# A low-rank adapter forward pass: the last software-queue store cut in three, and all software stores issued between casts

## The chip, the cores and the metric

The kernel runs on one core of one Trainium2 chip. The metric is device time in microseconds (us) of one launch. The kernel before took 161.09 us, the median of three runs (160.76 to 161.21).

## The reference

`x` has 16 x 2048 = 32,768 rows of 256 float32 values. The output has the same shape:

```
y = x_flat @ W                                   # W: 256 x 256
lora_out = ((x_flat @ lora_A) * lora_E) @ lora_B # rank 16
y = y + scale * lora_out                         # scale = 1.0
```

Since the adapter is linear, it can be folded into the weights once: `weff = W + lora_A @ diag(lora_E * scale) @ lora_B`. What is left is one product of 32,768 x 256 with 256 x 256. 33.55 MB of `x` come in and 33.55 MB of `y` go out.

## The kernel before

**Tiling.** The rows are cut into four chunks (0 to 3) of 8,192 rows. In a chunk each of the 128 partitions holds 64 consecutive rows (1 KB each) of `x`, so a whole chunk is 64 KB in every partition. An SBUF buffer named `ring` has three homes of that size. Chunk 3 uses the home of chunk 0 again, and a chunk's results overwrite its inputs in place.

**Transfers.** `sync_program` (line 142) goes through the list `ORDER` (line 18) on SyncE's queue, which is one of the hardware-driven queues and is called q1 in the profile. ("L", c, s, e) loads rows s to e of every partition of chunk c (line 155), and ("S", c, s, e) stores them (line 160). A load into a used home first waits for the stores that empty it (line 154). A store first waits for the count `s_done` (line 159). Here the stores are called by chunk: S0 (in two parts), S1, S2, S3. S2 covers only rows 2 to 62 of each partition's 64.

**Software stores.** The first two and last two rows of every partition of chunk 2 are left to GpSimd's software-driven queue, q0 in the profile. The helper `share` (line 163) stores them for a slice of partitions. `SHARES` (line 37) has three slices: partitions 108 to 112 (5 partitions), 0 to 107 (108 partitions) and 113 to 127 (15 partitions). A partition gives two pieces of 2 KB. GpSimd issues these stores at the end of its program (lines 198 to 200), after its last cast and a drain. All three add to one semaphore, `shared_stored`, and SyncE waits for it at line 161, after it has issued S3. The rest of the program's end (a barrier and the clearing of semaphores) follows, and the last wait of all, for S1, S2 and S3 to have landed, stands at line 308.

**Compute.** A cast (GpSimd, line 194) turns eight rows of every partition into bfloat16, in one of two `stage` buffers. There are 32 casts: numbers 0 to 7 are chunk 0, 8 to 15 chunk 1, 16 to 23 chunk 2 and 24 to 31 chunk 3. TensorE works in 64 groups of four rows: `turn` (line 243) transposes a group of a `stage` buffer into PSUM, VectorE copies that to SBUF (line 240), `multiply` (line 266) multiplies with `weff`, and ScalarE copies the product from PSUM into `ring` (line 217).

**Order around the change.** Cast n waits until TensorE has room for it (line 193: `s_room`, raised at the start of every second `multiply`). The first cast of chunk 2 also waits for the first part of S0 to have landed (lines 187 to 189). `s_done` (raised near the end of each `multiply`) is what SyncE waits for before a store. `(SHARED + 1) * ROWS // CG + NY` in line 198 is 50, which is the value that S2 waits for too: two groups past the last group of chunk 2.

Of the kernel before, what the change touches and what calls it, by code (L numbers as in the profile page):

```python
# [7 lines left out]
P = 128  # L8
# [5 lines left out]
ROWS = 64  # L14
# [19 lines left out]

SHARED = 2
END_ROWS = 2
SHARES = (slice(108, 113), slice(0, 108), slice(113, P))

HELD = (2, 0)
HOLDERS = (("S", 0, 0, 40),)  # L40
# [3 lines left out]
CG = 4  # L44
# [4 lines left out]
NS, NX, NT, NY = 2, 2, 2, 2  # L49
# [5 lines left out]
def kernel(  # L55
# [46 lines left out]
    shared_stored = sem("shared_stored")  # L102
# [12 lines left out]
    s_done = sem("rows_done")  # L115

    def rows(c, s, e):
        at = c % N_HOMES * ROWS
        return ring[:, at + s:at + e, :]

    sync, gpsimd, scalar, vector, tensor = nc.sync, nc.gpsimd, nc.scalar, nc.vector, nc.tensor
# [20 lines left out]
    def sync_program():  # L142
        for n, op in enumerate(ORDER):
# [14 lines left out]
            else:  # L158
                sync.wait_ge(s_done, -(-(c * ROWS + e) // CG) + NY)
                sync.dma_start(out=y_chunks[c, :, s:e, :], in_=at_home).then_inc(stored.get(op, stored_rest), 16)  # L160
        sync.wait_ge(shared_stored, 16 * len(SHARES))

    def share(engine, p, landed):
        def ends_of(at):
            return at[p].rearrange("p (q b) k -> p q b k", b=END_ROWS)[:, :: ROWS // END_ROWS - 1, :, :]

        engine.dma_start(out=ends_of(y_chunks[SHARED]), in_=ends_of(rows(SHARED, 0, ROWS))).then_inc(landed, 16)  # L167

    def gpsimd_program():
        gpsimd.memset(ident[:], 0.0).then_inc(s_ident, 1)  # L170
        gpsimd.wait_ge(s_ident, 1)
        gpsimd.affine_select(  # L172
            out=ident[:],
            in_=ident[:],
            compare_op=ALU.not_equal,
            fill=1.0,
            base=0,
            pattern=[[-1, P]],
            channel_multiplier=1,
        ).then_inc(s_ident, 1)  # L180
        n_casts = N_CHUNKS * ROWS // CAST
        for n in range(n_casts):
            c, b = n * CAST // ROWS, n * CAST % ROWS
            for op, landed in loaded.items():
                if op[1:3] == (c, b):
                    gpsimd.wait_ge(landed, 16)
            if (c, b) == HELD:
                for op in HOLDERS:
                    gpsimd.wait_ge(stored[op], 16)
            if n == 1:  # L190
                gpsimd.wait_ge(s_weff, 1)
            if n >= NS:
                gpsimd.wait_ge(s_room, n - NS + 1)  # L193
            gpsimd.tensor_copy(out=stage[n % NS][:], in_=rows(c, b, b + CAST)).then_inc(s_stage[n % NS], 1)  # L194

        gpsimd.wait_ge(s_room, n_casts - NS + 1)
        gpsimd.drain().then_inc(s_stage[n_casts % NS], 1)
        gpsimd.wait_ge(s_done, (SHARED + 1) * ROWS // CG + NY)
        for p in SHARES:
            share(gpsimd, p, shared_stored)  # L200

    def scalar_program():
        for name, to, of in (
# [108 lines left out]
    with tc.tile_critical(no_gpsimd_drain=True):  # L312
        sync_program()
        gpsimd_program()
        scalar_program()
        vector_program()
        tensor_program()
# [35 lines left out]
```

## Time and profile before

| what | value |
|---|---|
| median of 3 runs | 161.09 us (160.76 to 161.21) |
| the profiled execution's own time | 161.41 us |
| its span, from first to last instruction | 160.1 us |
| granted TensorE clock, mean | 0.823 |
| HBM read and written | 33.85 MB and 33.55 MB |
| mean DMA rate over the span | 421 GB/s |
| PE, ACT, POOL, DVE busy | 60%, 41%, 40%, 29% |
| 32 casts on GpSimd | 60.6 us busy, 1896 ns each |
| 3 software-store issues on GpSimd | 2.0 us, 675 ns each on average |

The span is the time from the first to the last instruction of one profiled execution, and that execution took 1.3 us more by the device's clock. In the views, q1 is SyncE's queue, q0 GpSimd's software queue, and an engine's name with a q behind it (SPq) is its sequencer, which waits and issues. "Landing" is the time from the issue of a transfer to its last completion.

### The profile page before, as it was taken

How to read it: one execution, taken by the hardware profiler on the slowest of the kernel's cores; microseconds unless marked ns; L12 is line 12 of the kernel's file. 1: busy time of each engine (PE TensorE's matmuls, PEld its weight loads, DVE VectorE, ACT ScalarE, POOL GpSimd, SP SyncE). 2: the span in 40 equal slices, each digit the busy share in tenths (PEclk: the TensorE clock that was granted, in tenths of full speed). 3: DMA queues.
4: the chain of work that ended last, by engine and by line, in shares of the span. 5: the costliest groups of instructions: out<-in, count | busy, mean ns of one | idle time of the engine just before them, and what ended most of it. 6: DMA issues, size and time to landing. Idle time of an engine off the chain costs nothing.

```text
span 160.1 us, 2042 instructions
## 1 busy us (share of the span) xinstructions
PE 95.3 (60%) x782; PEld 83.3 (52%) x782; DVE 46.1 (29%) x67; ACT 66.3 (41%) x66; POOL 63.3 (40%) x41
## 2 busy tenths in 40 slices
PE   2749999999999910000799999999993000000000
PEld 1235899999999900000699999999992000000000
DVE  0113355555555510000155555555551000000000
ACT  3000577777777730000077777777775000000000
POOL 1044676777767100003676768686850000000000
PEclk9999999999999985555599999999999555555555
DMA  7999999999979997989999999996997998999965
GB/s 270 426 442 436 411 446 434 475 401 401 598 311 524 442 344 328 481 348 442 430 461 393 475 434 401 524 491 295 524 462 308 481 484 354 480 432 390 523 295 248
DMA packets 2449, 67.41 MB, mean 421 GB/s; under 512 B 512, under 2 KB 528, under 8 KB 784
## 3 DMA queue, kind: packets, MB, share of 16 engines
q1 hardware_dynamic: 2016, 66.60, 97.2%
q0 software_dynamic: 224, 0.52, 0.9%
q10 hardware_dynamic: 208, 0.28, 0.5%
q14 instruction: 1, 0.01, 0.0%
HBM read 33.85 MB, written 33.55 MB: 421 GB/s over the span
## 4 chain that ended last, share of the span: by engine, by line
PE 41%; DMA 32%; POOL 2%; ACT 1%; issue 0%; SPq 0%; ACTq 0%; POOLq 0%
DMA out_dram<-ring 27%; PE psum_y L271 26%; PE psum_xt L251 14%; DMA ring<-in_x_dram 5%; POOL stage L194 2%; PE psum_y L297 1%; ACT ring L217 1%; SPq L146 0%; ACTq L217 0%; POOLq L193 0%
## 5 line engine op out<-in xcount | busy, mean ns | idle before, releaser
L217 ACT COPY ring<-psum_y 128x1024 f32 x64 | 64.8, 1013 | 54.3 <-PE psum_y L271 54.3
L194 POOL CAST stage<-ring 128x2048 bf16<-128x2048 f32 x32 | 60.6, 1896 | 52.8 <-DMA out_dram<-ring 22.1
L271 PE MATMUL psum_y<-weff,xt 128*128 128x256 bf16 x512 | 68.5, 278 | 0.0
L240 DVE COPY xt<-psum_xt 128x1024 bf16<-128x1024 bf16 x64 | 44.3, 691 | 62.9 <-PE psum_xt L251 62.9
L251 PE MATMUL psum_xt<-ident,stage 128*128 128x128 f32 x260 | 41.3, 283 | 23.4 <-POOL stage L194 23.4
L271 PEld LDWEIGHTS psum_y<-weff,xt 128*128 128x128 bf16 x512 | 51.3, 100 | 6.0
L251 PEld LDWEIGHTS psum_xt<-ident,stage 128*128 128x128 f32 x260 | 31.6, 146 | 26.3 <-issue 25.2
L283 PE MATMUL psum_y<-ident 128*128 128x512 f32 x4 | 3.8, 1101 | 2.9 <-POOL ident L172 2.9
L283 PEld LDWEIGHTS psum_y<-ident 128*128 128x128 f32 x4 | 1.2, 324 | 3.9 <-POOL ident L172 2.9
L167 POOL DMA_DIRECT2D out_dram<-ring x3 | 2.0, 675 | 1.5 <-PE psum_y L271 1.5
L222 DVE TENSOR_SCALAR stage<-psum_y,e_sb 16x256 f32<-16x256 f32 x1 | 0.5, 472 | 7.2 <-PE psum_y L289 7.2
L211 ACT ACT_TABLE_LOAD x1 | 1.3, 1283 | 2.1 <-SPq L312 2.1
L297 PE MATMUL psum_y<-stage 16*128 16x256 f32 x4 | 2.1, 670 | 0.0
L231 DVE COPY xt<-psum_xt 128x1024 bf16<-128x1024 bf16 x1 | 0.7, 692 | 3.8 <-PE psum_xt L251 3.8
L297 PEld LDWEIGHTS psum_y<-stage 16*128 16x128 f32 x4 | 1.2, 319 | 0.5 <-issue 0.3
L234 DVE TENSOR_TENSOR weff<-stage,psum_y 128x512 bf16<-128x512 f32 x1 | 0.7, 686 | 1.4 <-PE psum_y L297 1.4
L289 PEld LDWEIGHTS psum_y<-ident,a_sb 128*16 128x16 f32 x2 | 0.3, 137 | 1.2 <-issue 1.2
L170 POOL MEMSET ident<- 128x128 f32 x1 | 0.2, 205 | 1.7 <-SPq L312 1.7
L289 PE MATMUL psum_y<-ident,a_sb 128*16 128x128 f32 x2 | 0.6, 421 | 0.0
L172 POOL TENSOR_SCALAR_AFFINE_SELECT ident<-ident 128x128 f32<-128x128 f32 x1 | 0.3, 283 | 0.2 <-POOL ident L170 0.2
L211 ACT COPY one<-ident 128x1 f32<-128x1 f32 x1 | 0.2, 191 | 0.0
L334 POOL MEMSET const-float32-0.0<- 128x1 f32 x1 | 0.1, 93 | 0.2 <-issue 0.2
(3 smaller groups left out, 0.3 us busy)
## 6 DMA issues: line engine op xcount, KB each, us to landing
ring<-in_x_dram SPq DMA_DIRECT2D x4, 4096.0 KB, 24.6
out_dram<-ring SPq DMA_DIRECT2D x1, 7680.0 KB, 37.1
ring<-in_x_dram SPq DMA_DIRECT2D x2, 3072.0 KB, 17.0
out_dram<-ring SPq DMA_DIRECT2D x1, 5120.0 KB, 43.0
out_dram<-ring SPq DMA_DIRECT2D x1, 3072.0 KB, 42.7
ring<-in_x_dram SPq DMA_DIRECT2D x1, 2048.0 KB, 7.9
out_dram<-ring POOLq DMA_DIRECT2D x1, 432.0 KB, 31.3
stage<-in_W_dram ACTq DMA_DIRECT2D x1, 256.0 KB, 2.8
```

What stands on the lines that cost most here:

```text
L167: engine.dma_start(out=ends_of(y_chunks[SHARED]), in_=ends_of(rows(SHARED, 0, ROWS))).then_inc(landed, 16)
L194: gpsimd.tensor_copy(out=stage[n % NS][:], in_=rows(c, b, b + CAST)).then_inc(s_stage[n % NS], 1)
L211: scalar.copy(out=one[:], in_=ident[:, :1])
L217: scalar.copy(out=to, in_=psum_y[i % NY][:]).then_inc(s_free[(i + NY) % UNROLL], 1)
L231: vector.tensor_copy(out=xt[0][:], in_=psum_xt[0][:].bitcast(BF16)).then_inc(s_xt[0], 1)
L234: vector.tensor_add(out=weff[:], in0=w_sb, in1=psum_y[1][:, :KT, :]).then_inc(s_free[0], 1)
L240: vector.tensor_copy(out=xt[g % NX][:], in_=psum_xt[g % NT][:].bitcast(BF16)).then_inc(s_xt[g % UNROLL], 1)
L251: ins = tensor.transpose(psum_xt[i % NT][:, b, :], words[:, at * CG + b, :], ident[:])
L271: ins = tensor.matmul(psum_y[i % NY][:, b, :], xt[i % NX][:, b, t::KT], weff[:, t, :], start=(t == 0), stop=(t == KT - 1),)
L283: ins = tensor.matmul(psum_y[1][:, :2, :], ident[:], ident[:, None, :].to_broadcast([P, 4, P]), start=True, stop=True)
L289: ins = tensor.transpose(psum_y[0][:R, t, :P], a_sb[:, t, :], ident[:])
L297: ins = tensor.matmul(psum_y[1][:, t, :], ate[:, t, :], b_sb, start=True, stop=True)
```

## The change

`SHARES` gets five slices in place of three: the slice of the last 15 partitions is cut into three slices of 5. The stores keep their order: 5 partitions, 108 partitions, then 5, 5 and 5. They leave the end of GpSimd's program and go into its loop over casts: after cast 26 (the third of chunk 3) GpSimd waits for `s_done` to reach 50, and after each of casts 26 to 30 it issues one store. The wait of line 161 follows the number of slices, so it now asks for 80 in place of 48.

```
-SHARES = (slice(108, 113), slice(0, 108), slice(113, P))
+SHARES = (slice(108, 113), slice(0, 108), slice(113, 118), slice(118, 123), slice(123, P))
+FIRST_SHARE = 26
...
             gpsimd.tensor_copy(out=stage[n % NS][:], in_=rows(c, b, b + CAST)).then_inc(s_stage[n % NS], 1)
+            if n == FIRST_SHARE:
+                gpsimd.wait_ge(s_done, (SHARED + 1) * ROWS // CG + NY)
+            if 0 <= n - FIRST_SHARE < len(SHARES):
+                share(gpsimd, SHARES[n - FIRST_SHARE], shared_stored)
 
         gpsimd.wait_ge(s_room, n_casts - NS + 1)
         gpsimd.drain().then_inc(s_stage[n_casts % NS], 1)
-        gpsimd.wait_ge(s_done, (SHARED + 1) * ROWS // CG + NY)
-        for p in SHARES:
-            share(gpsimd, p, shared_stored)
```

## The prediction

> **What bounds the kernel now.** I read the page first: the slices and the queues.
>
> ```profile
> span 160.1 us, 2042 instructions
> ...
> DMA  7999999999979997989999999996997998999965
> ...
> q1 hardware_dynamic: 2016, 66.60, 97.2%
> q0 software_dynamic: 224, 0.52, 0.9%
> q10 hardware_dynamic: 208, 0.28, 0.5%
> ```
>
> The queues' packets fill 97.2 + 0.9 + 0.5 = 98.6% of 16 engines' span; no compute engine is above 60%. The DMA engines are the bound, and only 1.4% of 160.1 us, 2.2 us, is idle on the mean engine. Most of the low digits are packets over 2 us long, booked in one slice. The stretches of the end show it better (columns: length, then busy time of PE, PEld, DVE, ACT and POOL, clock, DMA share, GB/s).
>
> ```profile
> 123.00:139.00 16.00, 0.00 (x0) 0.00 (x0) 0.00 (x0) 0.00 (x0) 0.00 (x0) 0.53 1.00 429
> 139.00:155.00 16.00, 0.00 (x0) 0.00 (x0) 0.00 (x0) 0.00 (x0) 0.00 (x0) 0.50 1.02 435
> 155.00:160.00 5.00, 0.00 (x0) 0.00 (x0) 0.00 (x0) 0.00 (x0) 0.00 (x0) 0.50 0.49 211
> ```
>
> After 123 us nothing computes, and the DMA share is 1.00 and 1.02: full. What is on the queues there, and when it lands, comes from the DMA issues after 100 us (the last line is S3, issued at 122.84):
>
> ```profile
> out_dram<-ring SPq DMA_DIRECT2D x1, 7680.0 KB, 37.1
> out_dram<-ring POOLq DMA_DIRECT2D x1, 432.0 KB, 31.3
> out_dram<-ring POOLq DMA_DIRECT2D x1, 60.0 KB, 35.5
> out_dram<-ring POOLq DMA_DIRECT2D x1, 20.0 KB, 9.6
> out_dram<-ring SPq DMA_DIRECT2D x1, 37.2
> ```
>
> S2 is issued at 103.05 and lands 37.1 later, at 140.1. S3 is issued at 122.84, so it stands 17 us behind S2 in SyncE's queue before its own 20 us of packets run, and lands at 160.05, the end. The software stores, issued from 117.72, land at 127, 150 and 155. Last, the waits of SyncE after 100 us:
>
> ```profile
> SPq L146 <- DMA out_dram<-ring: 31.5, 1, 31.5
> ...
> SPq L308 <- SPq L308: 3.8, 1, 3.8
> ```
>
> The 31.5 us are the wait for the software stores (it ends at 154.7 us). After it comes the program's closing work, done at 156.3, and then 3.8 us of waiting for S3. So the software stores are not the end even now.
>
> **The trace's packet records** tell more. From 8 us on, each of the 16 engines starts a packet as the last one ends; I find no gap over 0.1 us. A 64 KB packet takes 2.418 us, one of 60 KB 2.267, one of 4 KB (both pieces of a partition) 0.159. The engines' last packets end between 158.3 and 159.7 us: one straggler at 159.7, which was already about 0.3 us behind at the first load (8.3) and fell 0.42 more behind at 99.7, the next at 159.1. The straggler's completion ends the kernel.
>
> **What the Trainium skill says.** *DMA: Bandwidth & Descriptors*, "Queues, rings and completion order": an engine goes round its queues packet by packet. The trace agrees: a 4 KB software packet stands after each SyncE packet. The same page, "Why a DMA increments its semaphore by 16 and not by 1": a software store of P partitions runs on the largest divisor of P up to 16, on consecutive engines from a cursor that moves on. The trace agrees: five engines have a data packet of the first store, twelve have nine of the 108-partition store, four have empty 8-byte packets instead, fifteen have one of the last. *Perfetto Trace Analysis*, "DMA Instruction — SWDGE (GPSIMD)": the recorded end of a software issue is when its descriptors are written, so it is GpSimd's cost. *SBUF — State Buffer*, "Who interferes with whom": a VectorE operation in a 2-port mode shuts GpSimd out of its port. The three issues of before ran at 564, 688 and 773 ns between VectorE copies, so no such block shows.
>
> **The change part by part.**
>
> 1. *Bytes per engine.* By the cursor, the first store is on engines 0 to 4, the 108 on 5 to 15 and 0, so 15 go on 1 to 15. After: 1 to 5, 6 to 10, 11 to 15. Partition 113 + j stays on engine 1 + j. Data packets per engine are unchanged: engines 1 to 4 have 2, the others 10. Zero.
>
> 2. *Two more stores.* The software queue's 224 packets are 128 data, 48 completions (3 x 16) and 48 empty ones (11 + 4 x 9 + 1). After: 128 + 80 + (11 + 36 + 33 = 80) = 288. The 64 extra at 9 ns over 16 engines: 64 x 0.009 / 16 = 0.04 us, on the path. Added.
>
> 3. *Moved DMAs.* The five stores' packets now go between those of S1 and S2 rather than S2 and S3. The first lands at about 103.2 + 9.6 = 113, the 108 at 105.8 + 31.3 = 137, the last at some 142. S1 and S2 land later by the packets let through first, at most 10 x 0.159 = 1.6 us an engine, most likely 0.6. Nobody waits for either before the end. Engines that are full do the same packets in another order: zero. This needs SyncE's queue never to run dry, which the next step checks.
>
> 4. *GpSimd.* The casts of chunk 3 show what room there is:
>
> ```profile
> 101.22 1.90 POOL L194 CAST stage<-ring 128x2048 bf16<-128x2048 f32 x1 [0.72 <-PE psum_y L271]
> 103.84 1.90 POOL L194 CAST stage<-ring 128x2048 bf16<-128x2048 f32 x1 [0.72 <-PE psum_y L271]
> 106.53 1.90 POOL L194 CAST stage<-ring 128x2048 bf16<-128x2048 f32 x1 [0.79 <-PE psum_y L271]
> ```
>
> Cast 26 is the first of these, ending at 103.12. The new wait is for 50, which released S2's issue at 103.05, so it costs nothing. The queued casts 27 to 31 each get one issue ahead: 0.56 to 0.77 us, and some 0.1 of dispatch, against 0.72 idle. So each pushes GpSimd by about 0.1, 0.5 us in all at most. TensorE needs cast 26 only at 104.54 (its transposes in the chain): 1.4 us after it was ready. That cover takes the 0.5: compute ends at 121 to 122 as before.
>
> 5. *S3's cover.* Were compute late, S3's issue would be. S2's first engine completes at 138.3; a small load shows 2.3 us from issue to landing, so S3 may be issued up to 138.3 - 2.3 = 136.0, or 13.2 us late, free. Without this cover every us of delay counts in full.
>
> 6. *The end.* The closing work now follows at about 142 to 144, and the last wait grows from 3.8 to some 16 us. It was hidden by S3 and stays so: zero.
>
> Sum: +0.04 us on the profiled execution: 161.41 to 161.45, span 160.1. That execution was 0.3 above the median of the runs, so on the median 161.09 + 0.04 = **161.1 us**.
>
> **The unknown.** The trace doesn't show software packets beside S1 while compute runs, nor what another interleaving does to slow packets. There are such: one of engines 1 to 4 takes 0.16 more on each of nine packets from 100 to 121 us, 1.4 in all; three others of the four lose 0.6 to 0.9 each from 136 to 149. Now they have a lead of 8 x 0.155 = 1.2 us for it, having eight data packets less. Bounds: if the straggler catches up, -0.6 (159.7 to 159.1); if an engine without a lead is hit, +0.6 to +1.4. I take zero, since the straggler's lag predates 103.
>
> **The rivals.**
>
> - *GpSimd starves (slower).* If an issue c is long among casts, compute is late by 5(c - 0.72) - 1.4, and S3 decides once this passes 13.2: c above 3.6 us, five times the 0.675 shown. At c = 4.5: 17.5 - 13.2 = +4.3, 165.4 us. The three measured issues, with VectorE running, speak against it; that none stood between casts is for it. Chance 0.03.
> - *Slow packets hit an engine without a lead (slower).* +0.6 to +1.4: 161.7 to 162.5. For it: such packets are in the trace. Against: seen mostly where an engine had a lead. Chance 0.09.
> - *The end gets more even (faster).* The straggler loses its lag: 160.5. Bounded by 0.6. Chance 0.07.
> - *The move does little, or the software stores are late after all* (the wait is met late, or packets queue up to S3): with some 16 us before the closing work binds, 161.1 too. Chance 0.05.
>
> **How the numbers follow.** Forecast 0.76; with the last rival, 0.81 for no change; slower 0.12, faster 0.07. Within 0.3% (0.48 us) is about what a measurement of this kernel can't tell from no change. The forecast alone spans 160.7 to 161.5, as the runs of before do. The range takes in the faster case and the milder end of the slow packets: 160.5 to 161.8.
>
> **What would show it.** Right: five issues of 0.5 to 0.8 us on GpSimd between casts, its idle time there near nothing; 288 packets on the software queue; S3 issued at 122 to 124; DMA share 1.0 from 123 to 155; the last wait some 16 us. Wrong: S3 issued after 136, gaps on the DMA engines, a 64 KB packet's time well above 2.42 us on the engine that ends last, or closing work after S3.

## The result, and the profile after

The changed kernel takes 167.9 us (median of five runs, 167.7 to 168.0) against 161.18 us for the kernel before in the same comparison. The ratio is 1.042, 95% interval 1.0404 to 1.0436. The prediction said 161.1 us and no change, so it was wrong. The profiled execution took 167.7 us with a span of 166.4 us, where the kernel before had 161.41 and 160.1. So 6.3 us have to be found in the span. Of all executions reported here one was far off (266.62 us, one of ten of the last experiment's kernel, for no known reason) and is left out of its ratio.

The page shows where to look first:

```profile
span 166.4 us, 2044 instructions
...
DMA  7999998989699799899998999969979991099965
...
q1 hardware_dynamic: 2016, 66.60, 93.5%
q0 software_dynamic: 288, 0.53, 0.9%
```

The same 66.60 MB now fill 93.5% of the engines' span rather than 97.2%, and slice 35 of 40 is a plain 0. The bound resource stands still there, which it never did before. The stretches put numbers to it (length, busy time of PE, PEld, DVE, ACT and POOL, clock, DMA share, GB/s), first for the kernel after:

```profile
122.00:138.00 16.00, 0.00 (x0) 0.00 (x0) 0.00 (x0) 0.00 (x0) 0.00 (x0) 0.56 1.05 447
138.00:146.00 8.00, 2.79 (x12) 1.91 (x12) 0.69 (x1) 1.01 (x1) 0.00 (x0) 0.50 0.33 136
146.00:166.00 20.00, 0.00 (x0) 0.00 (x0) 0.00 (x0) 0.00 (x0) 0.00 (x0) 0.50 0.85 367
```

The same eight microseconds in the kernel before:

```profile
138.00:146.00 8.00, 0.00 (x0) 0.00 (x0) 0.00 (x0) 0.00 (x0) 0.00 (x0) 0.50 1.00 426
```

From 138 to 146 us the DMA share falls from 1.00 to 0.33. The packet records name no engine, but after 8 us they fall into 16 chains in which a packet starts as the last one ends, one chain an engine. Each chain has one gap here, of 6.1 to 7.1 us, between its last packet of S2 or of the software stores and its first packet of S3. That accounts for the loss. Odder still, TensorE, VectorE and ScalarE do work in this stretch, some 20 us after compute ended in the kernel before. The chain of waits says what they had waited for:

```profile
118.85 0.44 PE psum_xt L253 x4
119.29 0.12 PE psum_y L273
119.41 21.36 POOLq L202
140.77 0.14 issue
140.91 1.09 PE psum_xt L253 x4
141.99 1.72 PE psum_y L273 x8
...
143.83 1.01 ACT ring L219
```

For 21.36 us TensorE stands behind GpSimd's line 202, `gpsimd.drain().then_inc(s_stage[n_casts % NS], 1)`. The call asks GpSimd to finish what it was given before, and then raises a semaphore. Its one instruction, in the kernel after:

```profile
L202 POOLq DRAIN  x1: 23946/23946/23946, 116.8 to 116.8; - x1
```

and in the kernel before, where it is line 197:

```profile
L197 POOLq DRAIN  x1: 46/46/46, 116.9 to 116.9; - x1
```

The same drain starts at the same time and takes 23,946 ns rather than 46. It ends at 140.76 us, 0.26 us after the last completion of the five software stores (140.50). Its increment lets TensorE do one more transposition of `stage` (line 251 of the kernel before, whose result nobody needs), and the program has that transposition stand ahead of the last `multiply`. So the last group of chunk 3 is some 21 us late, and with it `s_done`, and with that S3. The waits of SyncE after 100 us show it, first before, then after:

```profile
SPq L160 <- PEq L305: 19.4, 1, 19.4
```

```profile
SPq L161 <- PEq L307: 41.7, 1, 41.7
...
SPq L310 <- SPq L310: 19.0, 1, 19.0
```

SyncE waits 41.7 us rather than 19.4 for the count that releases S3, and issues S3 at 144.96 instead of 122.84. The engines had run out of other packets at 138.8 to 139.7. S3 then has the engines to itself and lands 21.4 us later, at 166.34:

```profile
out_dram<-ring SPq DMA_DIRECT2D x1, 7680.0 KB, 37.2
out_dram<-ring POOLq DMA_DIRECT2D x1, 432.0 KB, 29.7
out_dram<-ring POOLq DMA_DIRECT2D x4, 20.0 KB, 28.2
out_dram<-ring SPq DMA_DIRECT2D x1, 21.4
```

The part of GpSimd's queue that the prediction did look at behaves as it said:

```profile
101.13 1.90 POOL L195 CAST stage<-ring 128x2048 bf16<-128x2048 f32 x1 [0.72 <-PE psum_y L273]
103.23 0.69 POOL L168 DMA_DIRECT2D out_dram<-ring  x1 [0.21 <-issue]
103.92 1.90 POOL L195 CAST stage<-ring 128x2048 bf16<-128x2048 f32 x1
105.76 0.79 POOL L168 DMA_DIRECT2D out_dram<-ring  x1
```

The issues take 0.57 to 0.79 us and fit between the casts. The last cast starts at 114.23 here and at 114.33 in the kernel before.

### The profile page after: what moved, and what is told of

It is laid out like the page before. It is cut to its first block, busy times and chain, and to the rows that moved or that the text cites. A ratio compares the mean times of both kernels' runs of the same rounds, so it can differ in the third digit from the quotient of the medians.

```text
span 166.4 us, 2044 instructions
## 1 busy us (share of the span) xinstructions
PE 97.0 (58%) x782; PEld 84.2 (51%) x782; DVE 46.1 (28%) x67; ACT 66.3 (40%) x66; POOL 64.2 (39%) x43
## 3 DMA queue, kind: packets, MB, share of 16 engines
q1 hardware_dynamic: 2016, 66.60, 93.5%
## 4 chain that ended last, share of the span: by engine, by line
PE 40%; DMA 30%; POOLq 13%; POOL 2%; ACT 1%; issue 0%; SPq 0%; ACTq 0%
DMA out_dram<-ring 26%; PE psum_y L273 25%; PE psum_xt L253 14%; POOLq L202 13%; DMA ring<-in_x_dram 5%; POOL stage L195 2%; PE psum_y L299 1%; ACT ring L219 1%; SPq L147 0%; ACTq L219 0%; POOLq L194 0%
## 5 line engine op out<-in xcount | busy, mean ns | idle before, releaser
L273 PE MATMUL psum_y<-weff,xt 128*128 128x256 bf16 x512 | 69.5, 281 | 0.0
L253 PE MATMUL psum_xt<-ident,stage 128*128 128x128 f32 x260 | 42.0, 286 | 43.8 <-POOL stage L195 23.0
L168 POOL DMA_DIRECT2D out_dram<-ring x5 | 3.2, 641 | 0.2 <-issue 0.2
```

What stands on the lines that cost most here:

```text
L253: ins = tensor.transpose(psum_xt[i % NT][:, b, :], words[:, at * CG + b, :], ident[:])
L273: ins = tensor.matmul(psum_y[i % NY][:, b, :], xt[i % NX][:, b, t::KT], weff[:, t, :], start=(t == 0), stop=(t == KT - 1),)
```

## The experiments

The theory after the two traces, called the drain theory below: GpSimd's drain waits until every software store issued ahead of it has landed, and the last TensorE group waits for the increment on that drain. Rivals: the software packets between those of S1 and S2, or the issues between casts, cost the time; the larger number of stores does; or a drain among stores is dear by itself.

### The increment without the drain

```
-        gpsimd.wait_ge(s_room, n_casts - NS + 1)
-        gpsimd.drain().then_inc(s_stage[n_casts % NS], 1)
+        gpsimd.wait_ge(s_room, n_casts - NS + 1).then_inc(s_stage[n_casts % NS], 1)
```

> The changed kernel, with GpSimd's last drain replaced by a bare semaphore increment at the same place. Drain theory (the drain waits until the software stores issued ahead of it have landed, and TensorE's last group waits for its increment): S3 issued at about 122.7 us instead of 145, DMA engines without a gap, 161.1 us, within 0.3% of the kernel before. Traffic theory (software packets between those of S1 and S2, or issues between casts, are what costs): 167 to 168 us still.

Measured: 161.21 us, ratio 1.0001 (0.9986 to 1.0016), span 159.8. S3 is issued at 123.64, and the engines have no gap where they stood still:

```profile
138.00:146.00 8.00, 0.00 (x0) 0.00 (x0) 0.00 (x0) 0.00 (x0) 0.00 (x0) 0.50 0.92 398
146.00:158.00 12.00, 0.00 (x0) 0.00 (x0) 0.00 (x0) 0.00 (x0) 0.00 (x0) 0.50 1.01 438
```

(The 0.92 is how packets of 2.4 us are booked, to the stretch in which they start; the packet records have them back to back.) All five stores are still issued between the casts, and their packets still go among those of SyncE's stores. Neither the traffic nor the issues cost anything that can be measured. The whole 6.7 us went with one drain. From the start of cast 26 to the issue of S3 it is 21.6 us here (102.03 to 123.64) as in the kernel before (101.22 to 122.84), so the issues between the casts didn't make compute later.

### The drain kept, but watched by nobody

```
+        gpsimd.wait_ge(s_room, n_casts - NS + 1).then_inc(s_stage[n_casts % NS], 1)
+        gpsimd.drain()
```

These two lines stand in the place of the two that the first experiment removed.

> The changed kernel, with the increment ahead of the drain, so that nobody waits for the drain. Drain theory: the drain still takes some 24 us (116.8 to 140.7) and costs nothing: 161.1 us. A rival, that a draining GpSimd holds up the DMA engines themselves: 167 to 168 us.

Measured: 161.21 us, ratio 1.0001 (0.9982 to 1.0019). The drain is even longer here:

```profile
L202 POOLq DRAIN  x1: 30309/30309/30309, 117.6 to 117.6; - x1
```

It ends at 147.93, again just after the last software completion (147.67), and costs nothing. So a waiting drain doesn't hold up the DMA engines; what costs is the increment queued on it. The expected 24 us were too short, since S3's packets now stand between the last stores' packets and these land at 147.7 rather than 140.5.

### The cut undone, the move kept

```
-SHARES = (slice(108, 113), slice(0, 108), slice(113, 118), slice(118, 123), slice(123, P))
+SHARES = (slice(108, 113), slice(0, 108), slice(113, P))
```

> The changed kernel with the cut undone: three stores (5, 108 and 15 partitions) after casts 26 to 28, the drain in its place. Drain theory: the last store lands at about 140 as with five, so the drain ends at about 140 to 141 and the time is 167 to 168 us, ratio 1.038 to 1.044. If the number of stores were what counts (0.64 us an issue, more completions): 2 us or more under 167.9.

Measured: 167.36 us, ratio 1.0379 (1.0337 to 1.0421). The drain ends at 140.48, after the last completion at 140.30. Of the 6.7 us of the change, the move alone explains 6.2. Two stores fewer are worth 0.5 us by the medians, not 2, and the intervals of the two ratios overlap. The traces show half of it: S3 is issued at 144.68 rather than 144.96.

### The move undone, the cut kept

```
-SHARES = (slice(108, 113), slice(0, 108), slice(113, P))
+SHARES = (slice(108, 113), slice(0, 108), slice(113, 118), slice(118, 123), slice(123, P))
```

in the kernel before, with all five stores at the end.

> The kernel before with the cut alone: five stores, all issued at the end, after the drain. Drain theory: the drain takes 0.05 us, nothing waits for the stores but the closing work, 161.1 to 161.2 us (0.04 us for 64 more small packets). If more stores cost: slower by over 0.5 us.

Measured: 163.89 us, ratio 1.0161 (1.013 to 1.0193). This was a miss. It can't be the drain, which takes 46 ns. SyncE's waits after 100 us show another thing:

```profile
SPq L146 <- DMA out_dram<-ring: 36.8, 1, 36.8
SPq L160 <- PE psum_y L271: 20.1, 1, 20.1
SPq L160 <- PEq L305: 19.4, 1, 19.4
SPq L348 <- PEq L348: 1.5, 2, 1.2
```

The wait for the software stores is 36.8 us rather than 31.5, and the wait of line 308 for S3 (3.8 us in the kernel before) is gone from the list. The stores end at 160.06, S3 at 159.89, and the closing work now follows in the open until 162.32. The landings of the five stores tell why: 127.4, 149.8, 154.6, 159.4 and 160.1. Each small store behind the first two costs 4.8 us. In the packet records, a store puts two packets on each engine: one of data (or, where it has none, an empty one of 8 bytes) and one for the completion. Each stands behind one 2.42 us packet of SyncE's queue. If a round is one packet of each queue, a store takes two rounds, 4.8 to 5.0 us. The fifth is quick only because S3's packets have run out.

### Four stores at the end

```
-SHARES = (slice(108, 113), slice(0, 108), slice(113, P))
+SHARES = (slice(108, 113), slice(0, 108), slice(113, 121), slice(121, P))
```

> The kernel before with the last 15 partitions in two stores (8 and 7), so four stores, all at the end. Theory from the run with five at the end (on each DMA engine every store puts one completion packet, and here one data or empty packet, and each of these waits for one 2.4 us packet of SyncE's queue): the landings follow at 127, 150, 154.6 and 159.4 us, the last 4.8 us after that of before, and the closing work of about 2 us ends at 161.2 to 161.6: ratio 1.008 to 1.013. If five at the end was slow for another reason (512 KB cut into stores of 5 partitions, or GpSimd's issues): no more than 0.5 us from the kernel before, or about half of the 2.8 us.

Measured: 163.59 us, ratio 1.0151 (1.0136 to 1.0167). The landings are 127.3, 149.6, 154.4 and 159.5, as two rounds a store have it, and the closing work ends at 161.6:

```profile
out_dram<-ring POOLq DMA_DIRECT2D x1, 432.0 KB, 30.4
out_dram<-ring POOLq DMA_DIRECT2D x1, 32.0 KB, 34.5
out_dram<-ring POOLq DMA_DIRECT2D x1, 28.0 KB, 38.9
```

The landing times and the span met the expectation. The total did not quite: the profiled execution took 1.9 us beyond its span (163.49 against 161.6), where the kernel before takes 1.3. The run with five has 1.8 (164.09 against 162.3). Both end on the closing work rather than on the last store. Both also have a packet of 8 KB on the queue q14 (kind "instruction") that ends 0.8 to 1.1 us after the span, where in the kernel before it ends 0.6 us ahead of the span's end. Whether that is the 0.5 us outside the span, no run here shows.

### The stores just ahead of the drain, at the end

```
         gpsimd.wait_ge(s_room, n_casts - NS + 1)
-        gpsimd.drain().then_inc(s_stage[n_casts % NS], 1)
         gpsimd.wait_ge(s_done, (SHARED + 1) * ROWS // CG + NY)
         for p in SHARES:
             share(gpsimd, p, shared_stored)
+        gpsimd.drain().then_inc(s_stage[n_casts % NS], 1)
```

This is the kernel before with two statements exchanged.

> The kernel before with its three stores issued just ahead of the drain rather than behind it, all else at the end as before. Drain theory: issued at about 117, the last store lands some 29 to 38 us later (S3 no longer stands between its packets), so the drain ends at 146 to 155, S3 is issued 4.2 us after that and lands 21.4 later: 173 to 182 us. If the stores' place between casts were the cause: 161.1 us, since no cast follows them here.

Measured: 167.56 us (two executions), ratio 1.0405 (1.0384 to 1.0425). No cast stands behind a store here, and the time is within 0.4 us of the changed kernel's: the place between the casts is not the cause, the place ahead of the drain is. The drain ends at 140.55. The expected 173 to 182 us were wrong, and instructively so. Once S2 has run out (its engines complete at 138.3 to 139.6), nothing stands between the software packets any more, and what would have taken 10 us more takes one: the 108-partition store lands 21.6 us after its issue rather than 31.3, and the last at 140.4. The stall ends itself soon after the engines have nothing else to do. That fits with this kernel, the one with three stores moved and the changed one lying within 0.6 us of each other.

### Fewer stores ahead of the drain

Two runs change how long the drain waits. In the first, only the stores of 5 and of 108 partitions go between the casts and the other three are issued behind the drain:

```
-            if 0 <= n - FIRST_SHARE < len(SHARES):
+            if 0 <= n - FIRST_SHARE < 2:
                 share(gpsimd, SHARES[n - FIRST_SHARE], shared_stored)
 
         gpsimd.wait_ge(s_room, n_casts - NS + 1)
         gpsimd.drain().then_inc(s_stage[n_casts % NS], 1)
+        for p in SHARES[2:]:
+            share(gpsimd, p, shared_stored)
```

> The changed kernel with only the first two stores (5 and 108 partitions) between casts; the other three are issued behind the drain. Drain theory: the drain ends when the 108-partition store has landed, at about 135.6; S3 is issued 4.2 later, at 139.8, just too late to be covered by S2 (done at 139.3 to 139.7): some 1 us of gap on the DMA engines, 162.0 to 162.8 us. If the drain waited for a time by itself, or for the number of stores: about 165 to 168 us.

Measured: 162.59 us, ratio 1.0095 (1.0078 to 1.0112). The 108-partition store lands at 135.65 and the drain ends at 135.79:

```profile
L202 POOLq DRAIN  x1: 17612/17612/17612, 118.2 to 118.2; - x1
```

S3 goes out at 139.98, and the engines' gaps are 0.7 to 2.1 us. In the second run the slices are also changed, so that the store behind the first has 72 partitions and lands sooner:

```
+SHARES = (slice(108, 113), slice(0, 72), slice(113, 117), slice(72, 108), slice(117, P))
```

> As the run with 113 partitions ahead, but the second store has 72 partitions (6 packets on each of 12 engines rather than 9), and the other 51 partitions follow behind the drain in three stores. Drain theory: the 72-partition store lands at about 128, the drain ends there, S3 is issued at about 132.3, which S2 covers by 7 us: no gap on the DMA engines, 161.1 to 161.3 us, although the drain still takes some 11 us. If any drain of many us costs its length: 164 us or more.

Measured: 161.81 us, ratio 1.0045 (1.0028 to 1.0061). The drain ends at 128.89, after the landing at 128.75:

```profile
L202 POOLq DRAIN  x1: 11310/11310/11310, 117.6 to 117.6; - x1
```

S3 goes out at 133.09, ten microseconds late, and there is no gap on the engines: covered, as expected. Yet the time is 0.45% over the kernel before, which was not expected. The next run asks whether that came through S3's wait for the drain. In the kernel of this second run:

```
-        gpsimd.wait_ge(s_room, n_casts - NS + 1)
-        gpsimd.drain().then_inc(s_stage[n_casts % NS], 1)
+        gpsimd.wait_ge(s_room, n_casts - NS + 1).then_inc(s_stage[n_casts % NS], 1)
+        gpsimd.drain()
```

> The run with 77 partitions ahead of the drain, with the increment given ahead of the drain, so that S3 no longer waits for it and goes out at about 123. If the 0.45% of that run came through the drain: ratio 0.998 to 1.002. If they came from its stores' other layout on the DMA engines (slow packets, one engine with more of them): 1.003 to 1.006 as there.

Measured: 161.80 us, ratio 1.0039 (1.0025 to 1.0053), with S3 out at 124.13. So the residue doesn't come of S3's wait for the drain. It belongs to what these two kernels share: the layout of the stores, and the last three of them issued at about 130 us, behind the drain. Which of the two, no run shows. Their packet records have more slow packets: beyond their usual times, the packets of both queues after 100 us lose 12.2 us summed over 16 engines here and 11.7 in the run before, against 4.8 in the kernel before and 4.7 in the first experiment. About half of this is in the 4 KB packets of the software stores (6.2 and 5.4 us, against 1.1 and 1.2). The 7 us more are some 0.45 us an engine, by estimate, and the residue is 0.6 to 0.7 us. What makes packets slow was not found.

### The drain ahead of the first store

```
             if n == FIRST_SHARE:
                 gpsimd.wait_ge(s_done, (SHARED + 1) * ROWS // CG + NY)
+                gpsimd.drain()
...
-        gpsimd.wait_ge(s_room, n_casts - NS + 1)
-        gpsimd.drain().then_inc(s_stage[n_casts % NS], 1)
+        gpsimd.wait_ge(s_room, n_casts - NS + 1).then_inc(s_stage[n_casts % NS], 1)
```

> The changed kernel with the drain moved ahead of the first store (after cast 26), and the bare increment at the end. Drain theory: with no software store under way the drain takes about 0.05 us, and the time is 161.1 us. If the drain is dear by itself among casts: over 161.6 us.

Measured: 161.19 us, ratio 1.001 (1.0 to 1.002). The drain among the casts, with no software store under way, takes 134 ns:

```profile
L198 POOLq DRAIN  x1: 134/134/134, 104.4 to 104.4; - x1
```

### The runs side by side

| kernel | last landing ahead of the drain | drain ends | S3 issued | S3 landed | median |
|---|---|---|---|---|---|
| before | none | 116.96 | 122.84 | 160.05 | 161.18 |
| 77 partitions ahead | 128.75 | 128.89 | 133.09 | 160.53 | 161.81 |
| 113 partitions ahead | 135.65 | 135.79 | 139.98 | 161.37 | 162.59 |
| three stores moved | 140.30 | 140.48 | 144.68 | 166.07 | 167.36 |
| stores, then drain, at the end | 140.38 | 140.55 | 144.75 | 166.14 | 167.56 |
| changed kernel | 140.50 | 140.76 | 144.96 | 166.34 | 167.90 |
| drain watched by nobody | 147.67 | 147.93 | 123.46 | 160.02 | 161.21 |

In every line with a store ahead, the drain ends 0.14 to 0.26 us after the last landing. In the five lines where S3 waits for it, S3 goes out 4.2 us later: the transposition, the last `multiply`, the copy by ScalarE. (The granted clock of that stretch is 0.50 in the changed kernel, and the transposition takes 1.09 us there rather than 0.44.) In the last four of these, where S3 comes after S2 has run out, it lands 21.4 us after its issue. No kernel here beats the one before; the first, second and last experiments equal it.

## Why the prediction was wrong

**Step 4 failed, in its last sentence: "compute ends at 121 to 122 as before".** It named what is queued behind the moved issues, casts 27 to 31. But the drain of line 197 is queued there as well. In the kernel before it stood ahead of the three issues, in the changed one behind the five. It was priced at nothing by silence, although its 46 ns were measured with no software store under way. The runs put in its place: a drain behind a software store waits for that store's landing. It ended at 140.76 us, S3 went out 22.1 us late, and the time grew by 6.7 us.

**Step 3 failed with it: "Nobody waits for either before the end"** was right for S1 and S2, but the software stores themselves got a waiter, the drain, and through it TensorE and S3.

**Step 5 was right as a mechanism and nearly as a size.** It said that S3's issue may slip to 136.0, 13.2 us, for nothing. Issued at 133.09 it left no gap, at 139.98 gaps of 0.7 to 2.1 us. The first packets of S3 start 0.83 us after its issue (145.79 against 144.96), not the 2.3 us taken from a small load's landing, so by an estimate from this trace (138.8 less 0.83) the cover reaches to about 138. The slip was 22.1 us. The first rival, too, had the place right ("compute is late", "S3 decides once this passes 13.2"), but its cause wrong: the issues took 0.57 to 0.79 us, and none came near 3.6.

**Steps 1, 2 and 4 were right as far as they went.** There are 288 packets on the software queue. The wait for 50 cost nothing, and the issues took the time that step 4 gave them. With the drain's increment given freely, the very same stores at the very same places take 161.21 us, ratio 1.0001. So the forecast of no change holds for what it summed; the +0.04 us itself is too small to be told from nothing, as the interval is about 0.25 us to either side.

**Step 2 was right about load and left out latency.** By the prediction two more stores add 0.04 us of work to an engine, but each store behind others takes two rounds of 2.4 us. In the first experiment the last store landed at 147.75, not at "some 142" as step 3 had it. In the change itself little of this was left, since S2's packets had run out: the last landing was at 140.50 against 140.30 with three stores, and the medians differ by 0.5 us. At the end of the program the two stores are worth 2.8 us, since there the closing work loses its cover.

**Step 6, that the closing work stays hidden, was right,** but the 19.0 us of the last wait are no proof of its "some 16", since they come of a late S3. In the first experiment the last wait is 9.9 us, as the last store lands later than step 3 had it. The slow packets of "The unknown" did not decide; more of them than before appeared, beside a cost of 0.4%, only in the two runs with another layout. Two small misreadings of the prediction changed nothing: the three runs of the kernel before span 160.76 to 161.21 us (161.41 with the profiled execution), not 160.7 to 161.5, and its three software issues (117.72 to 119.73) ran in part at the same time as VectorE copies (118.12 to 118.81, 119.43 to 120.12), not between them.

## What to carry to other kernels

When an instruction that starts a transfer moves, look at what it moves past that waits for transfers, a drain above all, and then at who waits for that: a drain of 46 ns is a measurement of what was under way ahead of it. Where a drain is used only to carry a semaphore increment, put the increment on a plain semaphore instruction, as the first experiment does, or issue the stores behind the drain, as the kernel before does. And count a small store beside a busy queue in rounds as well as in bytes: with 2.4 us packets on the other queue, a store of one packet an engine waited for two of them.

## What the runs showed of the hardware

- GpSimd's drain waits for the landing of the software stores that it has issued, and ended 0.14 to 0.26 us after their last completion in seven kernels. It doesn't wait for SyncE's stores: with 77 partitions ahead it ended at 128.89, while S2 landed at 140.36. Without any under way it took 46 ns, or 134 ns right after a cast.
- A software store of one data packet an engine holds two turns on every DMA engine, on those without data for it too: one data or empty packet and one completion. Behind a full hardware queue of 64 KB packets that made 4.8 to 5.0 us a store. The Trainium skill (*DMA: Bandwidth & Descriptors*, "Queues, rings and completion order") has the engines go round packet by packet; the runs agree and add that an empty packet of 9 ns waits its turn like a full one.
- When the hardware queue ran dry, the remaining software packets went through within about one microsecond: S2's last packets in the changed kernel ended at 138.8 to 139.6, and its last two software stores landed at 140.2 and 140.5.
